# One more 4 KB buffer, one fewer turning buffer, and the row of x's factors moved into a gate buffer, in a one-core hybrid decoder layer

## The chip, the cores and the metric

The kernel runs on one core of a Trainium2 chip. The metric is the device time of one execution in microseconds (us), a median over executions. Engines are named as in the profile: PE is TensorE (matmul), PEld its weight loads, DVE VectorE, ACT ScalarE, POOL GpSimd, and SP the queue that issues every DMA of this kernel.

## What is computed

One decoder layer on `x` of 256 rows by 2048 columns, with 256 fixed memory rows `mem`, all in float32:

```python
h = rms_norm(x, g_mix)
qkv_a, z_a, b_a, a_a, q_b, k_b, v_b, f_b, q_m, gates = split(h @ w_in)
o_a = rms_norm(gated_delta_rule(conv_silu(qkv_a), ...)) * silu(z_a)     # 8 heads of 128, chunks of 64
o_b = forgetting_attention(rms(q_b), rms(k_b), v_b, log_f)              # 8 heads of 128
o_m = softmax_attention(rms(q_m), keys and values of rms_norm(mem))     # 4 heads of 256
y = sigmoid(gates)[a,b,m] * (o_a @ w_up_gdn, o_b @ w_up_fox, o_m @ w_up_mem), summed
x = x + y @ w_out
x = x + square(relu(rms_norm(x, g_mlp) @ w_ff1)) @ w_ff2                # 2048 -> 8192 -> 2048
```

## The kernel before

**Matmuls.** Every big product takes its weights in tiles of 1 MB (`wf`, four buffers). ACT rounds each half of a tile to fp32r (`whi`, L155), DVE makes the remainder (`wlo`, L156), and PE adds three products (L180 to L182): high by high, high by low, low by high. `gemm_a` works in steps of one weight tile: 24 matmuls of 512 columns. After each step it calls `tick()`, which advances every background generator in `bg` to its next `yield`. So the small work of the branches (the delta rule, both attentions, the transposes) is written between the steps of the big products. The framework orders the instructions of each engine when the program is built, with a priority that follows this written order (weights and evacuations are raised by `tc.high_priority`), and gives buffers out then; on the chip each engine runs its own list in order.

**Buffers.** Tiles with one tag share a fixed number of buffers, and a tile gets one when the last reader of its former holder is done. `t4` tiles (tag `s4`, pool of `N4` buffers of 4 KB a partition) hold almost everything large: the activations `h` (8 tiles), the memory branch's output `oM` (4), and in the delta rule, for each half `hf` of the heads, `kT`, `qT`, `vt`, `Ea`, `Mta`, `Ata`, `Mu`, `X`, `Ms`, `TTbd`, `Pbd`, `TT`, the gate `zt` and `o_tok`. `t2` tiles (tag `s2`, `N2` = 7 buffers of 2 KB) hold smaller ones, among them `Mtb`, `Atb`, `Tc`, `TTc`, `Pc`. `sm()` gives one of four PSUM banks, `acc()` one of the other four.

**The delta rule.** `gdn_chain(hf, st)` runs twice as a background generator. Its steps: products of keys with keys into `Mta`/`Mtb` (PE L618/L619, evacuated by DVE L621); DMAs of the diagonal blocks through DRAM into `Mu` (L632, L634); a memset of `X` (POOL L636); products of queries with keys, four PSUM banks, evacuated by L621 into `Ata`/`Atb`; 31 elimination steps on DVE, each an L645 (`Xt` from `Mu` and `X`) and an L647 (`X` from `Xt`); `X` out to DRAM (L651) and back as `Tc` (L653); `Ms` on POOL (L656), read by PE L667; on DVE `TTc` (L660), `TTbd` (L662); on PE L667 into a PSUM bank, copied to `Pc` and spread to `Pbd` (L671); on PE L676; `TT` (L683, L684); then L702, L697, L708, L713 for each of two time blocks. `TTbd` is written and read by nothing later.

**Turning.** `turned(src)` transposes 32x32 blocks on DVE into `ta` (L241), writes it to DRAM (SP L243), and loads it back turned as `tb` (SP L245). `ta` and `tb` share tag `turn`, `NT` = 4 buffers of 2 KB.

**The factors of x.** In `prep_x`, `dg` (a diagonal of 128 factors, tag `dg`, one buffer) is multiplied by ones on PE (L315) for each of two time blocks, and ACT copies the resulting row to `rbc` (L316, 1 KB of its own). `rbc` is read by DVE L266 while `h` is made, in the first 110 us. The `gt` tiles (two buffers of 2 KB) first hold gates in `combine`, after 690 us.

Of the kernel before, what the change touches and what calls it, by code (L numbers as in the profile page):

```python
# [9 lines left out]
F32 = mybir.dt.float32  # L10
# [5 lines left out]
P = 128  # L16
# [13 lines left out]
K_ID, K_ONE, K_GMASK, K_FMASK, K_M32, K_TBD, K_PBD, K_EV, K_OD, K_RST = (  # L30
    0, 128, 256, 640, 1024, 1152, 1156, 1160, 1161, 1162)
NCST = K_RST + 256
N4, N2, NT = 22, 7, 4
NWF, NHI, NLO = 4, 5, 5
XB = 3
PRI = 100
# [3 lines left out]
def body(ctx: ExitStack, tc: tile.TileContext, I, out, dbg=None):  # L40
    nc = tc.nc
    cp = ctx.enter_context(tc.tile_pool(name="cp", bufs=1))
# [3 lines left out]
    tp = ctx.enter_context(tc.tile_pool(name="tp", bufs=2))  # L46
# [7 lines left out]
    def nm(s):  # L54
        cnt[0] += 1
        return f"{s}{cnt[0]}"
# [4 lines left out]
    def t2(name, shape=(P, 2, 256), dt=F32):  # L61
        return s2p.tile(list(shape), dt, tag="s2", name=nm(name))
# [32 lines left out]
    def sm():  # L95
        return psm.tile([P, 512], F32, tag="sm", name=nm("sm"))
# [155 lines left out]
    def load_T(src, q):  # L252
        xt = t4("xt")
        nc.sync.dma_start(xt, src[:, q * 4:q * 4 + 4, :])
        return xt

    def split_scaled(dst, xt, q, gcol, rows=None, ks=range(4)):

        for k in ks:
            g = pk[:, gcol + q * 4 + k:gcol + q * 4 + k + 1]  # L260
            h, l = dst(q * 4 + k)
            if rows is None:
                A.activation(h, xt[:, k, :], AF.Copy, scale=g)
                V.scalar_tensor_tensor(l, xt[:, k, :], g, h.bitcast(F32), ALU.mult, ALU.subtract)
            else:
                V.scalar_tensor_tensor(xt[:, k, :], xt[:, k, :], g, rows, ALU.mult, ALU.mult)  # L266
                A.copy(h, xt[:, k, :])
                V.tensor_tensor(l, xt[:, k, :], h.bitcast(F32), ALU.subtract)

    def row_stats(name, src):  # L270

        ss = sp.tile([P, 2, 2], F32, name=nm(name))
        for tb in range(2):
            for i in range(2):
                xt = t4("xs", (P, 1024))
                nc.sync.dma_start(xt, src[tb][:, i * 1024:i * 1024 + 1024])
                A.activation(xt, xt, AF.Square, accum_out=ss[:, tb, i:i + 1])
            yield 1
        st = sp.tile([P, 2], F32, name=nm(name))
        V.tensor_reduce(st, ss, AX.X, ALU.add)  # L280
        V.tensor_scalar(st, st, 1.0 / D, EPS, ALU.mult, ALU.add)
        power(rstd[name], st, -0.5)
        yield 1

    rstd = {n: sp.tile([P, 2], F32, name="rstd_" + n) for n in ("m", "x")}
    rstd_m, rstd_x = rstd["m"], rstd["x"]
    rbc = cp.tile([P, 256], F32, name="rbc")
    mact, hact = Split("m", 16), Pairs("h", 16)


# [12 lines left out]
    def prep_x():  # L303
        nc.sync.dma_start(cst, I["cst"])
        yield 1
        for _ in row_stats("m", I["mem"]):
            yield 1
        for _ in row_stats("x", I["x"]):
            yield 1

        pr = sm()
        for tb in range(2):
            dg = tp.tile([P, 128], F32, tag="dg", name=nm("dg"), bufs=1)
            V.tensor_scalar(dg, ident, rstd_x[:, tb:tb + 1], None, ALU.mult)
            mm(pr[:, tb * 128:tb * 128 + 128], ones, dg, start=True, stop=True)  # L315
        A.copy(rbc, pr[:, :256])  # L316
        yield 1
        for q in range(4):
            xt = load_T(I["xT"], q)
            for i in range(2):  # L320
                split_scaled(hact, xt, q, C_GX, rbc, ks=(2 * i, 2 * i + 1))
                yield 1
# [51 lines left out]
    kTm = [t4("kTm") for _ in range(2)]  # L374
    vm = [t4("vm", (P, 2, 512)) for _ in range(2)]
    bg_prep = spawn(prep_x())
    for g in range(2):
        def ev(tb, ps, g=g):
# [700 lines left out]
```

## Time and profile before

| | |
|---|---|
| time, median of 3 executions | 1745.37 us (1742.57 to 1746.55) |
| time of the profiled execution | 1742.79 us |
| its span, first to last instruction | 1740.8 us |
| PE busy | 1712.3 us, 98% of the span |
| DVE, ACT, POOL busy | 62%, 48%, 3% |
| mean granted clock of TensorE | 0.996 |
| moved by DMA | 354.25 MB, mean 204 GB/s |

The span leaves out 1742.79 - 1740.8 = 2.0 us of the execution's own time. A busy share is an average over the whole span; where PE does not work is seen only by the list of its waits and by the timeline.

### The profile page before, as it was taken

The page shows a single profiled execution, that of the slowest core. Times are in us where ns is not written, and L with a number is a line of the kernel's source. Part 1 is how long each engine was busy: PE and PEld are TensorE (multiplying, and loading weights), DVE is VectorE, ACT ScalarE, POOL GpSimd, SP SyncE. Part 2 cuts the span into 40 slices and gives each one's busy share as a digit, 9 for nine tenths or more (in the row PEclk, how much of TensorE's full clock was granted, in tenths as well). Part 3 has the DMA queues.
Part 4 walks back from the last instruction along what each step waited for, and adds up shares of the span by engine and source line. Part 5 has one row for each costly group of instructions (what it writes and reads, how often), then busy time and mean ns, then how long its engine had stood idle before and what let it go on. Part 6 is the DMA issues. An engine that isn't in the chain of part 4 may idle for free.

```text
span 1740.8 us, 21324 instructions
## 1 busy us (share of the span) xinstructions
PE 1712.3 (98%) x8356; PEld 1441.1 (83%) x8356; DVE 1076.7 (62%) x1453; ACT 843.2 (48%) x1138; POOL 44.2 (3%) x45
## 2 busy tenths in 40 slices
PE   8999999988999999999999999999999999999999
PEld 6788888867878888888888888888888888888887
DVE  5767877986766556655566665654665556545653
ACT  6655755333455445544444554533553355334542
POOL 0000000011000000000000000000000000000000
PEclk9999999998999999999999999999999999999999
DMA  9866564653646566565668765555565455555562
GB/s 356 304 241 229 187 205 144 208 187 124 208 165 211 194 218 224 202 203 193 218 219 283 238 202 189 198 194 178 186 212 194 173 194 195 194 192 185 184 221 88
DMA packets 87124, 354.25 MB, mean 204 GB/s; under 512 B 15585, under 2 KB 38769, under 8 KB 49265
## 3 DMA queue, kind: packets, MB, share of 16 engines
q1 hardware_dynamic: 87024, 352.91, 59.2%
q8 instruction: 65, 1.06, 0.2%
q14 instruction: 35, 0.28, 0.0%
HBM read 337.66 MB, written 15.22 MB: 203 GB/s over the span
## 4 chain that ended last, share of the span: by engine, by line
PE 94%; DMA 2%; DVE 2%; issue 1%; ACT 1%; POOL 0%; SPq 0%; DVEq 0%; ACTq 0%
PE acc L180 21%; PE acc L182 21%; PE acc L181 21%; PE acc L230 21%; PE acc L208 7%; DMA tb<-turn 1%; DMA turn<-ta 1%; DVE wlo L156 1%; PE sm L618 0%; PE sm L421 0%; PE sm L565 0%; DMA cum_bc<-d_row 0%; PE sm L396 0%; DMA wf<-w_kv 0%; DVE ta L241 0%
## 5 line engine op out<-in xcount | busy, mean ns | idle before, releaser
L156 DVE TENSOR_TENSOR wlo<-wf,whi 128x1024 fp32r<-128x1024 f32 x594 | 719.5, 1225 | 533.4 <-ACT whi L155 532.7
L155 ACT CAST whi<-wf 128x1024 fp32r<-128x1024 f32 x594 | 616.2, 1050 | 683.5 <-PE acc L182 494.8
L230 PE MATMUL acc<-h,whi 128*128 128x512 f32 x1024 | 316.8, 395 | 0.0
L180 PE MATMUL acc<-whi,h 128*128 128x512 f32 x704 | 277.4, 394 | 0.7 <-ACT zt L901 0.7
L182 PE MATMUL acc<-whi,h 128*128 128x512 f32 x704 | 274.7, 390 | 0.0
L181 PE MATMUL acc<-wlo,h 128*128 128x512 f32 x704 | 274.7, 390 | 0.0
L230 PEld LDWEIGHTS acc<-h,wlo 128*128 128x128 f32 x1024 | 187.9, 188 | 42.4
L181 PE MATMUL acc<-wlo,uh 128*128 128x512 f32 x512 | 199.2, 389 | 0.0
L182 PE MATMUL acc<-whi,ul 128*128 128x512 f32 x512 | 199.2, 389 | 0.0
L180 PE MATMUL acc<-whi,uh 128*128 128x512 f32 x512 | 199.2, 389 | 0.0
L230 PE MATMUL acc<-h,wlo 128*128 128x256 f32 x1024 | 197.1, 279 | 0.0
L230 PEld LDWEIGHTS acc<-h,whi 128*128 128x128 f32 x1024 | 158.5, 189 | 2.8
L180 PEld LDWEIGHTS acc<-whi,h 128*128 128x128 f32 x704 | 132.6, 188 | 28.7 <-ACT zt L901 0.9
L182 PEld LDWEIGHTS acc<-whi,h 128*128 128x128 f32 x704 | 132.4, 188 | 28.0 <-issue 0.2
L181 PEld LDWEIGHTS acc<-wlo,h 128*128 128x128 f32 x704 | 132.6, 188 | 26.9
L208 PE MATMUL acc<-h,whi 128*128 128x512 f32 x384 | 137.2, 400 | 0.0
L182 PEld LDWEIGHTS acc<-whi,ul 128*128 128x128 f32 x512 | 96.1, 188 | 20.0
L181 PEld LDWEIGHTS acc<-wlo,uh 128*128 128x128 f32 x512 | 96.1, 188 | 20.0
L180 PEld LDWEIGHTS acc<-whi,uh 128*128 128x128 f32 x512 | 96.1, 188 | 20.0
L208 PE MATMUL acc<-h,wlo 128*128 128x256 f32 x384 | 103.6, 280 | 0.0
L208 PEld LDWEIGHTS acc<-h,whi 128*128 128x128 f32 x384 | 71.5, 188 | 14.9
L208 PEld LDWEIGHTS acc<-h,wlo 128*128 128x128 f32 x384 | 72.4, 189 | 1.7
(264 smaller groups left out, 1675.9 us busy)
## 6 DMA issues: line engine op xcount, KB each, us to landing
wf<-w_ff SPq DMA_DIRECT2D x128, 1024.0 KB, 4.8
wf<-w_gate SPq DMA_DIRECT2D x48, 1024.0 KB, 4.8
wf<-w_qkv SPq DMA_DIRECT2D x24, 1024.0 KB, 4.9
wf<-w_fox SPq DMA_DIRECT2D x24, 1024.0 KB, 4.8
wf<-w_up SPq DMA_DIRECT2D x24, 1024.0 KB, 4.8
wf<-w_out SPq DMA_DIRECT2D x16, 1024.0 KB, 5.0
wf<-w_kv SPq DMA_DIRECT2D x15, 1024.0 KB, 9.4
turn<-ta SPq DMA_DIRECT2D x42, 256.0 KB, 3.2
```

The source lines that it names most:

```text
L155: A.copy(hi, c)
L156: V.tensor_tensor(lo, c, hi.bitcast(F32), ALU.subtract)
L180: mm(ps[tb], xh[:, t], wh, start=(k == 0), stop=False)
L181: mm(ps[tb], xh[:, t], wl, start=False, stop=False)
L182: mm(ps[tb], xl[:, t], wh, start=False, stop=(k == nk - 1))
L208: mm(o, w, x, start=(k == 0 and i == 0), stop=(k == KT - 1 and i == 1))
L230: mm(o, w_, x, start=(k == 0 and i < 2), stop=(k == KT - 1 and i >= 2))
```

## The change

The pool of 4 KB buffers gets 23 instead of 22, the turning tag 3 instead of 4. `rbc` takes half of one of the two gate buffers instead of space of its own, and `dg` takes a 2 KB `s2` buffer for each time block instead of one buffer of its own. Per partition that is 4 KB more and 2 + 1 + 0.5 KB less. No computation is changed.

```diff
-N4, N2, NT = 22, 7, 4
+N4, N2, NT = 23, 7, 3
...
-    rbc = cp.tile([P, 256], F32, name="rbc")
+    rbc = tp.tile([P, 512], F32, tag="gt", name="rbc", bufs=2)[:, 0:256]
...
         for tb in range(2):
-            dg = tp.tile([P, 128], F32, tag="dg", name=nm("dg"), bufs=1)
+            dg = t2("dg", (P, 128))
             V.tensor_scalar(dg, ident, rstd_x[:, tb:tb + 1], None, ALU.mult)
             mm(pr[:, tb * 128:tb * 128 + 128], ones, dg, start=True, stop=True)
```

## Rows read from the trace of the kernel before

**Rows 1.** The page, busy time of each engine over the span.

```profile
PE 1712.3 (98%) x8356; PEld 1441.1 (83%) x8356; DVE 1076.7 (62%) x1453; ACT 843.2 (48%) x1138; POOL 44.2 (3%) x45
```

**Rows 2.** Waits of PE: line, releaser, us in total, times, longest.

```profile
PE sm L667 <- issue: 11.4, 1, 11.4
PE acc L180 <- ACT whi L155: 7.6, 1, 7.6
PE sm L822 <- ACT pTf L816: 1.0, 1, 1.0
```

**Rows 3.** Timeline of PE around the long wait: start, duration, idle before in brackets.

```profile
383.95 0.39 PE L182 MATMUL acc<-whi,h 128*128 128x512 f32 x1
395.78 3.59 PE L667 MATMUL sm<-Tc,Ms 128*128 128x32 f32 x16 [11.44 <-issue]
400.12 0.79 PE L180 MATMUL acc<-whi,h 128*128 128x512 f32 x1 [0.75 <-ACT zt L901]
...
403.19 0.39 PE L181 MATMUL acc<-wlo,h 128*128 128x512 f32 x1
403.42 0.39 PE L182 MATMUL acc<-whi,h 128*128 128x512 f32 x1
...
404.32 1.86 PE L676 MATMUL sm<-TTc,Pbd 128*128 128x32 f32 x16
```

**Rows 4.** Busy time by stretch: us, PE, PEld, DVE, ACT, POOL, clock, DMA.

```profile
384.00:395.80 11.80, 0.36 (x3) 0.05 (x1) 10.97 (x31) 1.04 (x1) 0.00 (x0) 0.73 0.29 106
395.80:403.10 7.30, 6.55 (x23) 5.84 (x24) 4.67 (x10) 1.35 (x3) 0.00 (x0) 0.50 0.08 18
403.10:420.00 16.90, 16.90 (x92) 13.96 (x92) 10.25 (x15) 6.86 (x9) 3.74 (x4) 1.00 0.42 130
420.00:498.00 78.00, 78.00 (x394) 65.02 (x393) 53.51 (x77) 37.78 (x62) 8.22 (x7) 1.00 0.60 198
```

**Rows 5.** Timeline of PE, the last products of queries and keys.

```profile
356.70 0.38 PE L619 MATMUL sm<-qT,kT 128*128 128x128 f32 x2
```

**Rows 6.** Timeline of DVE in the two delta-rule chains.

```profile
348.46 0.18 DVE L647 TENSOR_TENSOR X<-X,Xt 32x31 f32<-32x31 f32 x1
...
363.33 0.18 DVE L645 TENSOR_TENSOR Xt<-Mu,X 32x31 f32<-32x31 f32 x1 [1.07 <-DMA Mu<-dM]
...
394.72 0.18 DVE L645 TENSOR_TENSOR Xt<-Mu,X 32x31 f32<-32x31 f32 x1
394.94 0.48 DVE L621 SCALAR_TENSOR_TENSOR Ata<-sm,sc,Ea 128x256 f32<-128x256 f32 x1
...
397.55 0.43 DVE L660 STREAM_TRANSPOSE TTc<-Tc 128x256 f32<-128x256 f32 x1
...
400.85 1.23 DVE L671 TENSOR_TENSOR Pbd<-Pc,cst 128x1024 f32<-128x1024 f32 x1 [1.61 <-ACT Pc L669]
```

**Rows 7.** Timeline of ACT, the two evacuations of the gate z.

```profile
348.45 1.09 ACT L901 ACTIVATE zt<-acc 128x512 f32<-128x512 f32 x2 [5.20 <-DVE Xt L645]
...
399.47 1.08 ACT L901 ACTIVATE zt<-acc 128x512 f32<-128x512 f32 x2 [14.05 <-PE sm L667]
```

**Rows 8.** Timeline of SP, loads of `Tc` and `Mu`.

```profile
352.32 0.38 SPq L653 DMA_DIRECT2D Tc<-dX  x1
...
357.12 0.34 SPq L634 DMA_DIRECT2D Mu<-dM  x1
```

**Rows 9.** Timelines of SP and ACT, a pair of turned tiles.

```profile
492.92 0.38 SPq L245 DMA_DIRECT2D tb<-turn  x1
...
495.97 0.37 SPq L245 DMA_DIRECT2D tb<-turn  x1
...
499.33 0.52 ACT L816 COPY pTf<-tb 128x384 f32<-128x384 f32 x1
```

**Rows 10.** Timeline of ACT, the copy of the row of factors.

```profile
65.32 0.37 ACT L316 COPY rbc<-sm 128x256 f32<-128x256 f32 x1 [4.66 <-PE sm L315]
```

**Rows 11.** The page, the costliest group: busy us, mean ns, then idle before.

```profile
L156 DVE TENSOR_TENSOR wlo<-wf,whi 128x1024 fp32r<-128x1024 f32 x594 | 719.5, 1225 | 533.4 <-ACT whi L155 532.7
```

## The prediction

> **What bounds the kernel now.** I read the page first: PE is busy for 1712.3 us of 1740.8 [rows 1], so about 28 us are open to a change that adds and removes no matmul. Then the list of PE's waits [rows 2]: one wait of 11.4 us ahead of L667, one of 7.6 us at the very start for the first weights, and nothing else above 1.0 us. The reader should see that there is one place to win or lose something, and that "issue" as its releaser names nothing. The timeline around it [rows 3] and the table of stretches [rows 4] show what it costs: PE stops at 384.34 (383.95 plus 0.39), starts again at 395.78, and then works at a granted clock of 0.50, the lower of its two levels (1.2 GHz), until about 403.1. In the wait DVE is busy for 10.97 of 11.80 us [rows 4], so the question is what DVE does there and why PE needs it.
>
> The timeline of DVE answers [rows 6]. From 363.33 to 394.72 it runs the 31 elimination steps of the second chain, and only then the evacuations L621 of `Ata`/`Atb`, whose products were finished on PE at 356.70 plus 0.38 [rows 5]. Four products hold all four `sm` banks for those 38 us; L667 needs a bank, and starts 0.84 us after the first L621 begins (394.94 to 395.78). Why is L621 so late? `Ata` has no buffer. Counting the `t4` tiles alive at 341 us from the code: 8 `h`, 4 `oM`, `Ea` of half 1, both `vt`, `kT` and `qT` of half 1, both `Mta`, and of half 0 `Ata`, `Mu`, `X`: 22, all there are. The next tiles by first write are `zt`, `Ms`, `Mu`, `X`, `Ata`, `zt`, and the waits tell whose buffer each gets: the first `zt` waits 5.20 us for an L645, the last reader of the old `Mu` [rows 7]; the load of the new `Mu` is issued at 357.12, when the last reader of `kT` and `qT` is done [rows 5, 8]; L621 starts 0.04 us after the last L645 has read the new `Mu` [rows 6]; the second `zt` waits 14.05 us for L667, the last reader of `Ms` [rows 7].
>
> **The change part by part.** *23 buffers.* Each tile of that sequence moves up by one release: the first `zt` takes the extra buffer at once, `Ms` that of the old `Mu`, `Mu` that of the old `X`, and `X` and `Ata` those of `kT` and `qT` at 357. The eight L621 then run at 357 to 361 (four pairs of 0.48 and about 0.34 us), ahead of the elimination. All `sm` banks are free by 361, and the second `zt` takes the buffer of `Ea`, whose last readers are these same L621. What goes, term by term [rows 3]:
> - the wait ahead of L667: 11.44 us;
> - L667 at half clock: 3.59 us for 16 matmuls, where the same number of equal shape in L676 takes 1.86 at full clock: 1.73 us;
> - the wait for the second `zt`: 0.75 us;
> - seven matmuls from 400.12 to 403.19, 3.07 us, against a full-clock spacing of 0.23 (403.19 to 403.42), 1.6 us: 1.5 us.
>
> The sum is 15.4 us. The half clock goes with the wait, since the granted clock is 1.00 in the stretches after it [rows 4] and falls only here.
>
> What can eat into it: L676 needs `TTc` and `Pbd` from DVE, L702 needs `TT`. L667 is written three steps after the last product of queries and keys, and the five steps between 357.1 and 384.3 took 5.5 us each, so it comes at about 373.5, and L676 one step and 1.7 us later, at 380.7. Below: no wait, as `Tc` was loaded at 352.32 [rows 8] and DVE has over 5 us for a `Pbd` of 1.23 us [rows 6]. Above: if `TTc` stays behind all 31 elimination steps, which would end near 392 (they start some 3 us sooner), `Pbd` is ready at about 395 (0.43, then twice 1.23, `TTbd` taken as `Pbd`), and PE waits 14.3 us and loses some 3.2 us of clock: 17.5 us. I take 0: `TTc` runs directly after the L621 here, and not behind the last elimination step but in front of its L647, so what held it was the order of buffers behind `Atb`, and `Atb` now comes at 357.
>
> DVE must fit the 10.97 us of work that it did while PE stood still. It was busy for 10.25 of 16.90 us and 53.51 of 78.00 us in the stretches that follow [rows 4]: 31 us free, three times what is needed. Its splits of weights (1.2 us each [rows 11]) come once per half step and are written ahead. I take 0, between 0 and the 11 us that would be lost if none of it fitted.
>
> *Three turning buffers.* A pair of turned tiles needs at most three: at 495.97 the second load is issued while the first, of 492.92, is unread until 499.33 [rows 9], and each `ta` is given up when its own transfer to DRAM has ended, which is what the load waits for. I go by this for all of them. If two pairs meet, a load waits on SP until a tile is read, here 6.4 us after its issue (492.92 to 499.33), and weight loads queue behind it; they are issued up to four tiles, some 20 us of PE, ahead. Cost: 0, at most 6.4 us once.
>
> *`dg` and `rbc`.* Now ACT waits 4.66 us for the second small product [rows 10], which can come sooner with two `dg`; PE's own waits there are under 1.0 us [rows 2]. Gain 0, at most 1 us; loss 0, since the gate buffers are unused until 690 us.
>
> So the span becomes 1740.8 - 15.4 = 1725.4 and the execution 1727.4 us. The profiled execution lies 2.6 us below the median of the runs shown; carried over to that, 1730.0. I say **1729**, between the two.
>
> **The rivals.**
> 1. *The wait moves on to L676 or L702.* For it: DVE was full from 363 to 398, and PE arrives 22 us sooner at L667 (373.5 against 395.8). Against it: the place of `TTc` in rows 6. The wait can be anything from 0 to the 17.5 us above, so 1729 to 1747; the middle, half the gain, is 1738.
> 2. *Nothing changes.* The extra buffer could go to a tile written before the first `zt`, and the sequence stay as it is: 1745. Against it: every tile before `zt` had its buffer without any wait of PE, and a buffer more cannot make the sequence later. The Trainium skill, "Perfetto Trace Analysis", section "Optimization Strategy", takes a gap that repeats over a stretch of the busy engine as a sign that tiles find no space; this gap comes once [rows 2], so by that rule space would not be the limit and the time would stay at 1745. The chain of releasers above speaks against the rule here.
> 3. *Slower: the wait stays and PE runs into it sooner.* PE passed five steps between the products and L667, of which the code puts two behind L667: the order was made around a tile that was late. If the new order puts L667 at its written place and `Ata` still gets only the buffer of `Mu`, PE waits from 373.5 instead of 384.3, 10.9 us more: 1756. Each step that moves behind L667 costs 5.5 us, so one is enough to be slower. For it: DVE takes its list in order, and a list made for other durations is not corrected on the chip. That DVE's queue is a strict first-in-first-out is also stated by the Trainium skill, "PSUM — Partial Sum Buffer", section "Engine vs sequencer instructions"; the trace agrees, as `TTc`, with its load issued at 352.32, stood until 397.55 behind the work listed before it. Against it: `kT` and `qT` are given back by PE itself at 357, and with one buffer more two free ones meet two waiting tiles.
>
> **How the numbers follow.** The forecast gets 0.67, with a range of its own of 1724 to 1734 (up to 2 us more from the small waits and `dg`, up to 5 us of new waits). Rival 1 gets 0.15, of which 0.11 below 1742 and 0.04 above it; rival 2 gets 0.07, rival 3 0.11. What a measurement can tell from no change is 0.2%, 3.5 us: faster is below 1741.9, slower above 1748.9. Faster 0.67 + 0.11 = 0.78; same 0.04 + 0.07 = 0.11; slower 0.11. The range 1723 to 1742 holds the forecast and the lower part of rival 1, nearly 8 in 10, and its bounds are the small waits on one side and the 17.5 us of rival 1, mostly used, on the other.
>
> **What would show it.** Right: in the profile after, PE has no wait above 1 us but the first; the granted clock is 1.00 throughout 340 to 500 us; L621 into `Ata` runs within some 5 us of the last L619 on queries and keys, ahead of the elimination; the wait of POOL or ACT for L667 is gone, with the first `zt` no longer waiting for an L645. Rival 1 would show PE waiting ahead of L676 or L702 for DVE, with a stretch at half clock; rival 3 the same wait ahead of L667, longer. SP should show no load of `tb` waiting for a copy of another. The prediction is wrong if the order of the list on DVE keeps `TTc` behind the elimination, or if another tile stands between the extra buffer and `Ata`.

## The result and the profile after

The changed kernel takes 1723.69 us (median of 4 executions, 1722.12 to 1725.52), the kernel before 1744.57 us beside it (1742.57 to 1746.55): a ratio of 0.9881, with a 95% interval of 0.9864 to 0.9898. The forecast of 1729 was 5.3 us too high. The stated range of 1723 to 1742 holds the time by 0.7 us; the forecast's own narrower range, 1724 to 1734, misses it by 0.3. The profiled execution took 1723.02 us with a span of 1721.2, 19.6 us less than the span before.

The page, busy time of each engine over the span (to be read against [rows 1]):

```profile
PE 1708.4 (99%) x8356; PEld 1439.4 (84%) x8356; DVE 1076.9 (63%) x1453; ACT 847.6 (49%) x1140; POOL 44.6 (3%) x45
```

The waits of PE that are left: line, releaser, us in total, times, longest (against [rows 2]):

```profile
PE acc L180 <- ACT whi L155: 7.5, 1, 7.5
PE sm L502 <- DVE ct L485: 0.7, 1, 0.7
PE sm L502 <- DVE ct L490: 0.5, 1, 0.5
```

The wait ahead of L667 is gone, and so is that for the second `zt`. PE has the same 8356 matmuls, and its busy time is only 3.9 us shorter: that is the net of work that no longer runs at half clock and of some that newly does (the last section). The timeline of PE, small products of the second chain (against [rows 3, 5]):

```profile
355.55 0.38 PE L619 MATMUL sm<-qT,kT 128*128 128x128 f32 x2
...
372.15 1.86 PE L667 MATMUL sm<-Tc,Ms 128*128 128x32 f32 x16
...
379.42 1.86 PE L676 MATMUL sm<-TTc,Pbd 128*128 128x32 f32 x16
...
386.79 1.08 PE L702 MATMUL sm<-vt,TT 64*64 64x128 f32 x8
```

L667 comes 16.2 us after the last product, at full clock, and L676 and L702 follow at 7.3 and 7.4 us. Before, L667 came 38.7 us after the last product, and took 3.59 us.

That it was a PSUM bank that L667 lacked before can be read from what else it needs. `Tc` was loaded from 352.32 [rows 8], in 4.2 us, and `Ms` was written by 355.12, both long before PE stopped at 384.34. The bank came last: two L621 empty the first one, one into `Ata` at 394.94 [rows 6] and one into `Atb`, which ended at 395.68, and L667 started at 395.78. In the timelines of POOL and DVE of the kernel before:

```profile
352.85 2.27 POOL L656 TENSOR_TENSOR Ms<-Mtb,cst 128x512 f32<-128x512 f32 x1
...
395.34 0.34 DVE L621 SCALAR_TENSOR_TENSOR Atb<-sm,sc,Eb 128x128 f32<-128x128 f32 x1
```

The timeline of DVE in the same chain (against [rows 6]):

```profile
356.89 0.48 DVE L621 SCALAR_TENSOR_TENSOR Ata<-sm,sc,Ea 128x256 f32<-128x256 f32 x1
...
359.24 0.34 DVE L621 SCALAR_TENSOR_TENSOR Atb<-sm,sc,Eb 128x128 f32<-128x128 f32 x1
...
360.98 0.17 DVE L645 TENSOR_TENSOR Xt<-Mu,X 32x31 f32<-32x31 f32 x1
361.08 0.42 DVE L660 STREAM_TRANSPOSE TTc<-Tc 128x256 f32<-128x256 f32 x1
361.44 0.16 DVE L647 TENSOR_TENSOR X<-X,Xt 32x31 f32<-32x31 f32 x1
...
374.05 1.22 DVE L662 TENSOR_TENSOR TTbd<-TTc,cst 128x1024 f32<-128x1024 f32 x1 [1.00 <-PE sm L667]
375.19 1.22 DVE L156 TENSOR_TENSOR wlo<-wf,whi 128x1024 fp32r<-128x1024 f32 x1
376.33 1.22 DVE L671 TENSOR_TENSOR Pbd<-Pc,cst 128x1024 f32<-128x1024 f32 x1
```

The evacuations into `Ata` run ahead of the elimination instead of behind it: the first at 356.89 instead of 394.94. `TTc` follows at 361.08, before the first L647.

The timelines of ACT (the two evacuations of z) and of SP (the loads of `Tc` and `Mu`), against [rows 7, 8]:

```profile
335.22 1.08 ACT L901 ACTIVATE zt<-acc 128x512 f32<-128x512 f32 x2
...
360.79 1.28 ACT L901 ACTIVATE zt<-acc 128x512 f32<-128x512 f32 x2 [0.98 <-PE acc L182]
```

```profile
348.56 0.38 SPq L653 DMA_DIRECT2D Tc<-dX  x1
...
353.27 0.32 SPq L634 DMA_DIRECT2D Mu<-dM  x1
```

The first `zt` waits for no L645, the second only for its own product. `Mu` is loaded at 353.27, while the products of queries and keys still read `kT` and `qT`; before, it was loaded only after them.

The table of stretches (us, PE, PEld, DVE, ACT, POOL, granted clock, DMA share and GB/s):

```profile
340.00:420.00 80.00, 80.00 (x392) 66.29 (x390) 67.10 (x127) 31.79 (x37) 13.67 (x11) 1.00 0.54 182
420.00:498.00 78.00, 78.00 (x402) 65.64 (x401) 52.43 (x78) 42.48 (x67) 3.69 (x4) 1.00 0.62 206
```

**Where the 19.6 us came from.** The same matmul can be found in both traces, and its two starting times subtracted. Where both kernels have run the same matmuls up to it, the difference is a lead. Three such L180, one between the products and L667, one after the stall, one after 500 us; in the timeline of PE of the kernel before:

```profile
369.21 0.39 PE L180 MATMUL acc<-whi,h 128*128 128x512 f32 x1
...
412.77 0.39 PE L180 MATMUL acc<-whi,h 128*128 128x512 f32 x1
...
520.78 0.39 PE L180 MATMUL acc<-whi,h 128*128 128x512 f32 x1
```

and in that of the changed kernel:

```profile
368.07 0.39 PE L180 MATMUL acc<-whi,h 128*128 128x512 f32 x1
...
396.09 0.39 PE L180 MATMUL acc<-whi,h 128*128 128x512 f32 x1
...
501.69 0.39 PE L180 MATMUL acc<-whi,h 128*128 128x512 f32 x1
```

The lead is 1.14 us ahead of the stall, 16.68 behind it and 19.09 after 500 us; the last L180 of all leads by 19.44. So the stall itself gave 15.54 us, the stretch around 500 us 2.41, the rest 0.35, and the 1.14 was there before.

### The profile page after: what moved, and what is told of

It reads as the page before. It is cut to its first block, busy times and chain, and to the rows that moved or that the text cites. A ratio compares the mean times of both kernels' runs of the same rounds, so it can differ in the third digit from the quotient of the medians.

```text
span 1721.2 us, 21338 instructions
## 1 busy us (share of the span) xinstructions
PE 1708.4 (99%) x8356; PEld 1439.4 (84%) x8356; DVE 1076.9 (63%) x1453; ACT 847.6 (49%) x1140; POOL 44.6 (3%) x45
## 4 chain that ended last, share of the span: by engine, by line
PE 98%; DVE 1%; DMA 0%; issue 0%; ACT 0%; SPq 0%; DVEq 0%
PE acc L180 22%; PE acc L181 22%; PE acc L182 22%; PE acc L230 21%; PE acc L208 7%; PE sm L618 0%; PE sm L421 0%; PE sm L565 0%; PE sm L396 0%; DMA wf<-w_kv 0%; PE sm L708 0%; PE sm L702 0%; PE sm L822 0%; PE sm L726 0%; PE sm L713 0%; PE sm L619 0%
## 5 line engine op out<-in xcount | busy, mean ns | idle before, releaser
L180 PE MATMUL acc<-whi,h 128*128 128x512 f32 x704 | 277.0, 393 | 0.0
L180 PE MATMUL acc<-whi,uh 128*128 128x512 f32 x512 | 199.2, 389 | 0.0
L180 PEld LDWEIGHTS acc<-whi,h 128*128 128x128 f32 x704 | 132.2, 188 | 27.4 <-issue 0.3
L180 PEld LDWEIGHTS acc<-whi,uh 128*128 128x128 f32 x512 | 96.1, 188 | 19.9
```

What stands on the lines that cost most here:

```text
L180: mm(ps[tb], xh[:, t], wh, start=(k == 0), stop=False)
```

## The experiments

Times beside each are medians; the ratio is to the kernel before, run on the same chip beside it (1742.57 us beside the diagonals alone, the two turning buffers and the last two runs, 1742.99 beside the other four).

**The other edits without the buffer.** The changed kernel with:

```diff
-N4, N2, NT = 23, 7, 3
+N4, N2, NT = 22, 7, 3
```

> The changed kernel with 22 instead of 23 buffers of 4 KB; three turning buffers, the row of factors in a gate buffer and dg in an s2 buffer stay. Theory A (Ata of the second half waits for a 4 KB buffer, and its four products keep PE out of the sm banks): the wait ahead of L667 is back, some 11 us with some 3 us at half clock, the two waits near 500 us too; only the 1 to 2 us around 60 us stay gained; 1741 to 1744 us. Theory B (a new order of the list, whatever caused it, or the smaller tags, removed the wait): 1724 to 1730 us, no wait ahead of L667.

Measured: 1742.01 us, ratio 0.9996 (0.9987 to 1.0005). PE's waits, and the first L621 on `Ata` in the timeline of DVE:

```profile
PE sm L667 <- issue: 11.7, 1, 11.7
```

```profile
394.64 0.48 DVE L621 SCALAR_TENSOR_TENSOR Ata<-sm,sc,Ea 128x256 f32<-128x256 f32 x1
```

The wait is back in full and `Ata` is again behind the elimination. The three other edits together can't be told from no change: theory A held, and B, by which they matter, fell.

**A buffer for `Ata` of half 1 alone.** 22 shared buffers, and one more that only this tile may use:

```diff
-N4, N2, NT = 23, 7, 3
+N4, N2, NT = 22, 7, 3
...
+        At = (t4("Ata") if hf == 0 else tp.tile([P, 4, 256], F32, tag="Ata1", name=nm("Ata"), bufs=1),
+              t2("Atb", (P, 4, 128)))
```

> As e1, with 22 buffers, and one 4 KB buffer that only Ata of the second half uses. Theory A: that is the one tile that must not wait, so the wait ahead of L667 goes as it did with 23, though the first zt still waits some 5 us for the last reader of the old Mu; 1723 to 1727 us. Theory B': it was the first zt, at the head of the line of waiting tiles, that kept ACT and so PE back; then a buffer for Ata alone leaves a wait of PE of 5 us or more; 1730 to 1742 us.

Measured: 1723.25 us, ratio 0.9891 (0.9877 to 0.9904), the changed kernel's time within the scatter. The timelines of PE, DVE and ACT (lines are one further down in this kernel):

```profile
372.24 1.86 PE L668 MATMUL sm<-Tc,Ms 128*128 128x32 f32 x16
...
350.39 0.48 DVE L622 SCALAR_TENSOR_TENSOR Ata<-sm,sc,Ea 128x256 f32<-128x256 f32 x1
...
347.20 1.08 ACT L902 ACTIVATE zt<-acc 128x512 f32<-128x512 f32 x2 [5.00 <-DVE Xt L646]
```

Here only `Ata` of half 1 got a buffer, and the tiles ahead of it in the line got none. The first `zt` still waits 5.00 us for the old `Mu`, nearly as before (5.20 [rows 7]), and PE does not wait at L668 (L667 in the other kernels). So it was the lack of a buffer for `Ata` that PE paid for: theory A again, against B'. `Ata` is written even sooner than in the changed kernel (350.39 against 356.89), which gives nothing more.

**No buffer more, but another order.** The kernel before, with the products of queries and keys written ahead of the load of `Mu` and the memset of `X`, so that `Ata` asks for its buffer first:

```diff
+        for hs in ((0, 1), (2, 3)):
+            products(At, qT, hs)
+            yield 1
...
-        for hs in ((0, 1), (2, 3)):
-            products(At, qT, hs)
-            yield 1
```

> The kernel before, with its 22 buffers and all its tags, but the products of queries and keys are written ahead of the loads of Mu and the memset of X. Ata then stands ahead of Mu and X in the line for buffers; kT and qT, which come free with these products, go to Mu and X. Theory A: no buffer more is needed, the wait ahead of L667 goes: 1724 to 1732 us; the elimination may start later and leave a wait of up to 5 us further on. Theory C (22 buffers are too few for this stretch, whichever tile is last in line): a wait of about the same length appears at another place; 1738 to 1748 us.

Measured: 1727.58 us, ratio 0.9908 (0.9895 to 0.9922), with no wait ahead of L667. So 22 buffers are enough to be rid of the stall, which came from who asked first; theory C fell. The list of PE's waits has five that the changed kernel does not have, 4.2 us in all (1.3, 1.0, 0.8, 0.7 and 0.4), of the 5.0 us by which its span is longer (1726.2 against 1721.2). The timelines of PE and of DVE:

```profile
372.88 1.87 PE L667 MATMUL sm<-Tc,Ms 128*128 128x32 f32 x16
...
401.08 1.97 PE L676 MATMUL sm<-TTc,Pbd 128*128 128x32 f32 x16
```

```profile
357.61 0.48 DVE L621 SCALAR_TENSOR_TENSOR Ata<-sm,sc,Ea 128x256 f32<-128x256 f32 x1
...
361.81 0.43 DVE L660 STREAM_TRANSPOSE TTc<-Tc 128x256 f32<-128x256 f32 x1
...
397.53 1.23 DVE L662 TENSOR_TENSOR TTbd<-TTc,cst 128x1024 f32<-128x1024 f32 x1
...
399.80 1.22 DVE L671 TENSOR_TENSOR Pbd<-Pc,cst 128x1024 f32<-128x1024 f32 x1
```

The tiles that now come late are `TTbd` (which nothing reads) and `Pbd` behind it, with the end of the elimination. That is what the first rival feared; but L676 stands at 401.08 in PE's list here, behind big products, and the list of PE's waits has none ahead of it.

**The diagonals alone.** The kernel before with one edit of the change:

```diff
-            dg = tp.tile([P, 128], F32, tag="dg", name=nm("dg"), bufs=1)
+            dg = t2("dg", (P, 128))
```

> The kernel before with one edit alone: the two diagonals of factors take a 2 KB buffer each; 22 buffers of 4 KB, four turning buffers and the row of factors as before. Theory D1 (the edit with the diagonals is worth its two waits near 60 us and no more, and keeps the wait ahead of L667): waits 11.4 to 11.7 us ahead of L667; matmuls after 68 us come 1.2 to 2.7 us sooner than in the kernel before; 1741 to 1743.5 us, unless half clock elsewhere takes it back. Theory D2 (what was gained by 68 us in the changed kernel came from the row of factors in the gate buffer or from chance at the start): matmuls after 68 us within 0.6 us of the kernel before; 1744 to 1745.5 us.

Measured: 1742.36 us, ratio 1.0001 (0.9992 to 1.001). The timeline of PE, two lines with a wait, in the kernel before:

```profile
61.12 0.50 PE L181 MATMUL acc<-wlo,mh 128*128 128x512 f32 x1 [0.84 <-DVE wlo L156]
...
63.62 0.49 PE L315 MATMUL sm<-dg,cst 128*128 128x128 f32 x2 [0.39 <-DVE dg L314]
```

and the four small products with the diagonals alone:

```profile
61.69 0.61 PE L315 MATMUL sm<-dg,cst 128*128 128x128 f32 x4
```

Both waits go, and the L180 at 69.28 us starts at 66.49, a lead of 2.8 us. Of this 0.7 was there at 14 us: PE's first matmuls start 0.43 us apart, and they go over to 0.23 us apart at 12.7 us here and at 14.1 in the kernel before (the granted clock reads 1.00 there in both). The other 2.1 us came with the diagonals, 0.9 more than the two waits. The lead does not last: it is 1.2 us at 168 us and nothing by the end (spans 1740.8 and 1740.8). The table of stretches shows who took it. In the kernel before:

```profile
163.00:166.40 3.40, 2.32 (x13) 1.76 (x14) 3.34 (x17) 2.90 (x8) 0.00 (x0) 1.00 0.45 141
...
396.00:406.00 10.00, 9.25 (x44) 8.31 (x45) 4.47 (x10) 2.40 (x4) 0.00 (x0) 0.65 0.06 13
```

and with the diagonals alone:

```profile
163.00:166.40 3.40, 3.40 (x12) 2.88 (x12) 3.40 (x7) 0.16 (x1) 0.00 (x0) 0.52 0.46 98
...
396.00:406.00 10.00, 9.25 (x36) 7.96 (x35) 3.53 (x7) 2.39 (x4) 0.00 (x0) 0.54 0.06 13
```

PE works at half clock around 163 to 166 us, where before it did not, and longer behind the stall (0.54 against 0.65). Theory D1 held for the gain by 69 us (2.8 us in all, just above its 2.7; 2.1 of it from the edit), and its last clause for the time, which cannot be told from that of the kernel before beside it (1742.57); D2 fell.

**One diagonal in the changed kernel.** The reverse test:

```diff
-        for tb in range(2):
-            dg = t2("dg", (P, 128))
+        dg = t2("dg", (P, 128))
+        for tb in range(2):
```

> The changed kernel, with one dg tile for both time blocks, so that the second is written when PE has read the first, as before the change. If the 2 us that the changed kernel is ahead by at 62 us come from the two dg tiles: the waits of PE of 0.8 and 0.4 us near 60 us are back, and the time is 1724.5 to 1726.5 us, 1 to 2 us more than the changed kernel. If they come from the other edits or from chance in the start: no such wait, 1723 to 1724.5 us.

Measured: 1728.17 us, ratio 0.9912 (0.9898 to 0.9925), 4.5 us above the changed kernel where 1 to 2 were expected, so neither theory's range holds it. PE's waits, in a profiled execution that was the slowest of five (1730.91 us, the others 1726.41 to 1729.43):

```profile
PE acc L181 <- DVE wlo L156: 2.4, 1, 2.4
PE acc L180 <- ACT yh L370: 2.0, 1, 2.0
PE sm L822 <- ACT pTf L816: 1.3, 1, 1.3
```

Only the first stands near the edit, at 65 to 68 us, in place of the two that were expected. The other two are at 491 and 944 us, and there every engine runs the same instructions in the same order as in the changed kernel: the last difference of order is at 246 us, on DVE. So they are not from a new order; what made them is not shown. By 313 us this kernel is 2.4 us behind the changed one, and 7.7 at the end, so most of what it lost came far from the edit, and its time does not measure the diagonal. The run before it reads the diagonal at its place.

**Two turning buffers.** The changed kernel with:

```diff
-N4, N2, NT = 23, 7, 3
+N4, N2, NT = 23, 7, 2
```

> The changed kernel with two turning buffers instead of three. If three are what a pair needs (the reading of rows 9 in the prediction), two make the second load wait until the first turned tile has been read: each wait on SP at most 6.4 us, weights are issued some 20 us ahead, so it shows as waits of SP but costs PE at most a few us: 1723 to 1729 us. If turned pairs never overlap, no wait at all and 1723 to 1724 us. If SP's wait does hold up weight loads, PE waits for wf or whi after 480 or 940 us and the time is above 1729 us.

Measured: 1724.33 us, ratio 0.9904 (0.9888 to 0.992). SP's waits ahead of the loads of turned tiles, in this kernel and then in the changed one:

```profile
SPq L245 <- DMA turn<-ta: 39.6, 38, 4.8
...
SPq L245 <- ACT qTm L353: 1.7, 1, 1.7
```

```profile
SPq L245 <- DMA turn<-ta: 39.0, 35, 4.7
```

One load waits for a tile to be read, for 1.7 us at 155 us; the other waits are those for the way to DRAM, 0.6 us more in all. Every engine's list is in the same order as in the changed kernel. PE has three small waits that the changed kernel does not have (0.6, 0.3 and 0.2 us), none of them for weights, and the span is 1.1 us longer (1722.3 against 1721.2), which is within the scatter of the times. So two buffers cost next to nothing here, and the prediction's price of 0 for going from four to three holds with room to spare.

**Products first, with the other edits and with everything.** Two runs: 22 buffers, three turning buffers, the new diagonals and the row in a gate buffer, with the products ahead of `Mu` (first); and the changed kernel with that order too (second). The edits are those shown above.

> 22 buffers of 4 KB with the change's other edits (three turning buffers, two diagonals, the row of factors in a gate buffer), and the products of queries with keys written ahead of the load of Mu. Theory A (the stall is only Ata behind Mu; the other edits are worth about 2 us near 60 us): no wait ahead of L667, and 2 us below the kernel with products first alone: 1724 to 1727 us. Rival: the small edits are worth nothing by themselves, since what they give is taken back by half clock elsewhere: 1727 to 1729 us.

> The changed kernel with the products of queries with keys written ahead of the load of Mu as well. Theory A: both cures remove the same wait, so together they give no more than one: 1722.5 to 1725 us, and PE's waits remain the first one of 7.5 us and small ones of about 1 us in all. Rival: with both, the elimination starts later and Tc, TTc and Pbd with it, so a wait of PE comes ahead of L676 or L702: 1726 us or more.

Measured: 1727.82 us, ratio 0.9913 (0.99 to 0.9927), for the first, so theory A of it fell and the rival held: the small edits give nothing beside products first alone (0.9908) either. For the second 1724.07 us, ratio 0.9892 (0.9878 to 0.9905): two cures of one stall give no more than one, and no wait comes ahead of L676 or L702. Its small waits are 2.1 us in all, where about 1 was expected. One of PE's waits in the first of the two:

```profile
PE acc L180 <- ACT yh L370: 2.0, 1, 2.0
```

PE waits 2.0 us for a copy of `y` there, 1.3 with products first alone, and not at all in the changed kernel; it is one of the places in which the kernels with products first and 22 buffers lose their 4 us to the changed one.

## Why the prediction was right

**The bound and the cause.** The step that carried the prediction was that four `sm` banks stay full because `Ata` has no 4 KB buffer until the new `Mu` is released. Three runs show it from three sides: without the buffer the wait is back (11.7 us), with a buffer for `Ata` alone it is gone, and with `Ata` asking ahead of `Mu` it is gone without any buffer.

**The sequence of buffers.** Which buffer a tile takes is not in the profile, but each sign that was named came: L621 on `Ata` at 356.89 to 359.24 (357 to 361 forecast), `TTc` at 361.08 ahead of the elimination's first L647, no `zt` waiting for an L645 or for L667, `Mu` loaded before the last product. L667 came at 372.15 and L676 at 379.42 (373.5 and 380.7 forecast, from a kernel that lay 1.1 us later at this point).

**The terms.** The sum for the stall and its half clock was 15.4 us; 15.54 were measured. The clock was 1.00 throughout 340 to 498 us. The rest of the 19.4 us, 3.9, are side terms that the sum left at nothing and the forecast's own range allowed up to 2 us:
- around 500 us 2.4 us: two waits of 0.73 (L697) and 1.05 (L822, 1.0 in [rows 2]) that the sum left in place are gone; the other 0.6 us is not assigned. Both waits stay without the buffer (0.7 and 0.8) and with products first (0.7 and 1.0), where the stall is gone, so they do not hang on the stall. That of L697 is there in all five kernels that have the 22 shared buffers and no more, and in none of the five that have one more; PE runs the products around it in another order in the two groups. That of L822 is between 0 (changed) and 1.3 us (one diagonal) in the same order, so the order alone does not set it; what does was not traced. This is the term that makes most of the 4.2 us by which the span's forecast of 1725.4 was too high.
- ahead of the stall 1.1 us: 0.6 are there at 14 us, from the passage from 0.43 to 0.23 us between matmuls, which came sooner (in the kernel without the buffer this lead is 0.1), and the other 0.5 is, by difference, what is left of the diagonals.
- around 944 to 960 us 0.35, of which 0.26 is a wait for `yh`.

So the size of the main term was right by its mechanism. That the time stayed within the stated range, by 0.7 us, is in part luck: the range starts 6 us below 1729, and the prediction names 2 us of small waits and `dg` for it, where the side terms gave 3.9.

**The diagonals and the row of factors.** Priced at 0, at most 1 us. The local gain was larger, 2.1 us at 69 us (2.74 less the 0.62 from the start), and the net gain of the diagonals alone is what was priced: nothing that can be measured. The reason given (PE's own waits there are under 1.0 us) missed both the local gain and the half clock elsewhere that took it back, so here the price was right by luck.

**The turning buffers.** Priced at 0, and 0 was found; the reading behind it, that a pair needs at most three, was careful, since two cost less than can be told.

**DVE and the rivals.** DVE did fit its 11 us: it is busy for 67.10 of 80.00 us from 340 to 420, and PE waits for it nowhere in that time. The slack was smaller than forecast: `Pbd` ended at 377.55, 1.9 us ahead of L676, because `TTbd` and a split of weights stand between L667 and it. `TTbd`, which reads nothing of L667, still waits 1.00 us for it, the last reader of `Ms`, so with 23 buffers the pool is still full there. Rival 1 did not come, though its mechanism showed with products first, where `TTbd` and `Pbd` ended behind the elimination. Rival 2 fell with the time. The Trainium skill, "Perfetto Trace Analysis", section "Optimization Strategy", says that a gap which repeats can mean that the next tile finds no space. It says nothing against that reading for a gap that comes once, so the prediction took more from it than it states: here a single gap of 11.44 us closed with one buffer. Rival 3 fell too: L667 did return to its place 16 us behind the products, as it said, but with the banks free.

**Between the profile and the median.** Of the 5.3 us by which 1729 was too high, 4.4 lie between the execution summed, 1727.4, and the profiled one, 1723.02. Another 1.6 were added to come from the profiled execution to the median, where the measured median lies only 0.7 above the profiled execution.

## What to carry to other kernels

When the busy engine waits once, for nothing that the profile names, look for who holds its PSUM banks, which evacuation would free them, and whose last reader that evacuation follows: a full bank can be the sign of a missing SBUF buffer. Which tile waits for a buffer is decided by who asks first, so moving the request of the tile whose lack blocks PSUM banks ahead of those that can wait is worth trying before memory is found for another buffer (here 1727.6 against 1723.7 us, from 1743). A gain of 2 us read at one place of a trace is not a gain of the kernel: look at the same matmul further on, and at the end.

## What the runs showed of the hardware

The clock took back gains. In the changed kernel PE waits for 0.65 and 0.47 us ahead of L502, as it did before. The table of stretches of the changed kernel:

```profile
160.00:163.00 3.00, 1.84 (x12) 1.19 (x11) 2.94 (x16) 3.00 (x9) 0.00 (x0) 0.98 0.31 117
163.00:166.40 3.40, 3.40 (x12) 2.92 (x12) 3.40 (x7) 0.40 (x1) 0.00 (x0) 0.51 0.45 116
166.40:180.00 13.60, 13.60 (x79) 11.82 (x79) 11.80 (x19) 8.58 (x12) 0.00 (x0) 1.00 0.67 227
```

The granted clock is 0.51 in the stretch from 163.0 to 166.4 us, behind the waits, though PE is busy throughout it; 0.50 is the lower level (1.2 GHz). In the kernel before the same two waits are followed by 1.00. All seven kernels with the new diagonals and no wait of PE near 60 us show the fall behind these waits (changed, without the buffer, own buffer, diagonals alone, two turning buffers, both with products first). The two with the old diagonal and waits near 60 us do not (before, products first), nor does the one with a single diagonal, where the clock fell behind the wait of 2.4 us instead. The table of stretches of that one:

```profile
69.00:72.40 3.40, 3.40 (x10) 2.69 (x9) 3.40 (x6) 0.74 (x2) 0.00 (x0) 0.53 0.41 142
163.00:166.40 3.40, 2.24 (x13) 1.45 (x11) 3.31 (x16) 3.39 (x8) 0.00 (x0) 1.00 0.46 151
```

So a wait of a given length does not have one price: behind the same 1.1 us of waits the kernel with the diagonals alone lost 1.6 us (its lead of 2.8 us at 69 us is 1.2 at 168) that the kernel before did not lose. What decides it stays open.
